# Gate and up products grouped by weight half, splits and additions pinned behind the mixers' chains, two loads held back, and a narrower last tile

## The chip, the cores and the metric

One core of one Trainium2 chip runs the whole program in a single launch. The metric is the device time of that launch in microseconds. Engines are named as in the profile: PE is TensorE (PEld its weight loads), DVE is VectorE, ACT is ScalarE, POOL is GpSimd, SP is SyncE, whose queue issues nearly all DMA transfers.

## The reference

A decoder trunk of two layers over one sequence: T = 256 tokens, D = 1024, all in float32. Each layer is a mixer and a SwiGLU network, each with a residual addition and an RMSNorm ahead of it; a last RMSNorm ends it.

```python
def rmsnorm(x, g):
    y = x * rsqrt(mean(x * x, -1) + 1e-6)
    return y * g
for layer in range(2):
    h = rmsnorm(x, norm_mix[layer])
    x = x + (even_mixer if layer == 0 else odd_mixer)(h)   # projection, attention branches, output projection
    h = rmsnorm(x, norm_ffn[layer])
    x = x + (silu(h @ w_gate) * (h @ w_up)) @ w_down       # D_FF = 2816
out = rmsnorm(x, norm_final)
```

The even mixer joins sparse attention with differential attention (two softmax maps a head, subtracted). The odd mixer joins compressed, selected and sliding-window attention in 16 heads of 64.

## The kernel before

**Products in halves.** Every large product is made from float32 numbers split into a high part `hi` (the value copied to the format fp32r) and a low part `lo` (the rest). A projection adds three products, hi·hi, hi·lo and lo·hi: `mm3`, lines 381 to 383 in the profile. In the gate and up products the activations stand side by side, 256 columns of hi and 256 of lo, in the tile `aW`. One product with the high weights (line 489) is therefore 512 wide, and one with the low weights (line 490) 256 wide, over the high columns only.

**Weights.** Class `Weights` brings the weights in tiles of 512 KB (`w_raw`, 4 buffers, by SP's queue, in the order of the program). ACT copies a tile to its high half `w_hi` (line 122) and DVE subtracts that to get `w_lo` (line 125); hi and lo have 7 buffers each. A tile of the gate or up weights holds 4 of the 8 steps over D, for 256 columns. `W.next()` hands out the next tile and makes splits some tiles ahead; `W.load` issues the transfers.

**The network (`ffn`).** Gate and up run in 11 chunks of 256 columns: 2 banks of gate (`ps_g`), 2 of up (`ps_u`), each bank 8 steps over D. Per step and bank comes one product of line 489 and one of line 490, in turn. After a chunk ACT and DVE add the two column halves, scale them (`rB`), apply Silu, multiply (`sg`, `hn`, lines 498 to 503) and split the result (`hT_hi`, `hT_lo`). `residual` then multiplies down, adds to x (line 435) and feeds the next norm.

**`residual` and `Norm`.** `residual` also makes the mixers' output projections. It runs over the last `tail` weight tiles bank by bank, so that the four quarters of x (two token tiles t by two column halves h) end one after the other. `amid` is called after the first quarter: in the even mixer it turns and splits the last attention output. After each quarter DVE adds to x (line 433, or 435 with a scale), `Norm.half` multiplies by the gain (`xg`, line 302), PE turns it (`pt_a`, line 278), and ACT and DVE split it into `aW` (lines 271, 272). `gain(...)` allots one shared buffer for a norm's gain and issues its transfer (line 203) on SP's queue; the buffer's last reader has to be done.

**Ends of the mixers.** In the odd mixer the last group of heads goes score, softmax (`softmax_terms`, lines 451 and 452), scaling by the sum (`e`, line 974), transposes (`pt_p`, line 979), products with the values (`ps_o`), split (`aT`). `cws`, a small table, is loaded at its head (line 784).

**`Final`.** It squares each quarter on ACT with a running sum (line 366), adds and takes the power −1/2 (DVE line 255, POOL), and scales the two output halves on ACT (line 375) and DVE (line 377).

**What sets the order.** The Tile framework's scheduler orders each engine's instructions by data and priority. `pin` (keep_in_program_order) fixes the order among the pinned. An engine works through its list in order, so an instruction that waits holds all behind it.

Of the kernel before, what the change touches and what calls it, by code (L numbers as in the profile page):

```python
# [15 lines left out]
D = 1024  # L16
# [65 lines left out]
class Weights:  # L82


    def __init__(self, tc, pool, rpool, lead, flats, specs, ahead, bufs, spare):
# [9 lines left out]
        self.ready = []  # L95
        self.used = 0

# [7 lines left out]
    def prepare(self, upto, behind=False, before=None):  # L105

        nc = self.tc.nc
        while len(self.ready) < min(upto, len(self.queue)):
# [8 lines left out]
            o = 0  # L117
            for j, part in enumerate(raw):
                if before:
                    before(j, len(raw))  # L120
                c = slice(o, o + part.shape[-1])
                act = nc.scalar.activation(hi[:, c], part, AF.Copy)  # L122
                if behind:
                    self.tc.keep_in_program_order(act)
                nc.vector.tensor_sub(lo[:, c], part, hi[:, c])  # L125
                o = c.stop
# [11 lines left out]
def trunk(tc, x, lead, w0, w1, sm0, cw, vec, cst, out, dbg=None):  # L138
# [107 lines left out]
    def evac(dst, src):  # L246
        A.activation(dst, src, AF.Copy)
# [21 lines left out]

    def split(hi, lo, src):  # L270
        A.activation(hi, src, AF.Copy)  # L271
        V.tensor_sub(lo, src, hi)  # L272

    def split_T(dst, k0, src, n, behind=False):

        pt = t_bank("pt_a").rearrange("p (k c) -> p k c", k=4)
        for i in range(n):
            mmi = TE.transpose(pt[:, i], src[:, i * P : (i + 1) * P], ident)
            if behind:
                pin(mmi)  # L280
        split(dst[0][:, k0 : k0 + n], dst[1][:, k0 : k0 + n], pt[:, :n])

    class Norm:


        def __init__(self, goff):
            self.goff = goff
            self.wide, self.aT = new_wide()
            self.rs = [small_tile(1, "rs") for _ in range(NT)]
            self.last = None  # L290
            self.ms = [None] * NT

        def finish(self):

            if self.last is not None:
                split_T(self.aT[NT - 1], 4, self.last, 4, behind=True)
                self.last = None

        def half(self, t, h):
# [3 lines left out]
            if (t, h) == (NT - 1, 1):  # L303
                self.last = xg
            else:
                split_T(self.aT[t], 4 * h, xg, 4)
# [48 lines left out]
    class Final:  # L355


        def __init__(self):
            self.ms = [small_tile(2, "ms2") for _ in range(NT)]
            self.y = [[nat("y") for _ in range(2)] for _ in range(NT)]  # L360

        def half(self, t, h):
            ms = self.ms[t]
            c = slice(512 * h, 512 * h + 512)
            sq = ap.tile([P, 512], BF16, tag="sq", bufs=2, name="sq")
            A.activation(sq, xs[t][:, c], AF.Square, scale=1.0 / math.sqrt(D), accum_out=ms[:, h : h + 1])
            V.tensor_mul(self.y[t][h], xs[t][:, c], gains[V_FIN][:, c])
            if h == 1:
                rf = small_tile(1, "ms")
                rsqrt_sum(rf, ms)  # L370
                for h in range(2):
                    c = slice(512 * h, 512 * h + 512)
                    y = self.y[t][h]
                    if h == 0:
                        A.activation(y, y, AF.Copy, scale=rf)
                    else:
                        V.tensor_scalar(y, y, rf, None, op0=ALU.mult)
                    (A, nc.sync)[h].dma_start(out[t * P : (t + 1) * P, c], y)

    def mm3(ps, act, k, wh, wl, start, stop):  # L380
        TE.matmul(ps, act[0][:, k], wh, start=start, stop=False)  # L381
        TE.matmul(ps, act[0][:, k], wl, start=False, stop=False)  # L382
        TE.matmul(ps, act[1][:, k], wh, start=False, stop=stop)  # L383
# [17 lines left out]
    def residual(act, nk, tail, nxt, rs=None, amid=None):  # L401

        ps = [[mm_bank("ps_out") for _ in range(2)] for _ in range(NT)]

        def one(t, h, k, wt):
            c = slice(512 * h, 512 * h + 512)
            mm3(ps[t][h], act[t], k, wt[0][:, 0, c], wt[1][:, 0, c], k == 0, k == nk - 1)
# [7 lines left out]
        if amid:  # L415
# [5 lines left out]
        for t, h, k0, k1 in order:  # L421
            c = slice(512 * h, 512 * h + 512)
            for k in range(k0, k1):
                one(t, h, nk - tail + k, last[k])
# [7 lines left out]
            if rs is None:  # L432
                V.tensor_add(xs[t][:, c], ps[t][h], xs[t][:, c])
# [15 lines left out]
    def softmax_terms(pool, s, m, scale, bias, e, den, n):  # L449

        V.tensor_tensor_reduce(e, s, m, -scale, 3e38, ALU.add, ALU.min, bias)  # L451
        A.activation(e, e, AF.Exp, scale=-1.0, bias=bias, accum_out=den)  # L452

    def ffn(nm, goff):
        wide, rs = nm.wide, nm.rs
        gain(goff)
        nxt = Final() if goff == V_FIN else Norm(goff)
        with tc.tile_pool(name="ffn", bufs=1, side="left", reuse_waits="tile") as fp:
# [18 lines left out]
            for w in FF_CHUNKS:  # L477
# [4 lines left out]
                for dst in (gp, up):  # L482
                    for g in range(KD // kk):
                        wh, wl = W.next()
                        for i in range(kk):
                            k = g * kk + i
                            for f in range(nf):
                                c = slice(f * P, (f + 1) * P)
                                TE.matmul(dst[f], wh[:, i, c], wide[:, k].rearrange("p z q -> p (z q)"), start=k == 0, stop=False)  # L489
                                TE.matmul(dst[f][:, :T], wl[:, i, c], wide[:, k, 0], start=False, stop=k == KD - 1)  # L490
# [14 lines left out]
                f0 += nf  # L505
            hT = [[z[:, :, t * P : (t + 1) * P] for z in (hh, hl)] for t in range(NT)]
# [665 lines left out]
```

## Time and profile before

| | |
|---|---|
| time, median of 3 runs | 659.0 us (657.96 to 659.56) |
| profiled execution | 660.14 us, span 658.4 us, mean granted clock 0.996 |
| even mixer, with its output projection | 0 to about 138 us |
| gate and up of the first network | 138 to about 263 us |
| down of the first network | to about 324 us |
| odd mixer, with its output projection | to about 466 us |
| gate and up of the second network | to about 590 us |
| down of the second network, and the end | to 658.4 us |

The profile is of one execution, and all places in it are in microseconds from the start of its span. "Busy" is the time in which an engine executes; products on PE overlap, so the step from one product's start to the next one's is what a product costs in a stream, and not its own duration.

### The profile page before, as it was taken

The page shows a single profiled execution, that of the slowest core. Times are in us where ns is not written, and L with a number is a line of the kernel's source. Part 1 is how long each engine was busy: PE and PEld are TensorE (multiplying, and loading weights), DVE is VectorE, ACT ScalarE, POOL GpSimd, SP SyncE. Part 2 cuts the span into 40 slices and gives each one's busy share as a digit, 9 for nine tenths or more (in the row PEclk, how much of TensorE's full clock was granted, in tenths as well). Part 3 has the DMA queues.
Part 4 walks back from the last instruction along what each step waited for, and adds up shares of the span by engine and source line. Part 5 has one row for each costly group of instructions (what it writes and reads, how often), then busy time and mean ns, then how long its engine had stood idle before and what let it go on. Part 6 is the DMA issues. An engine that isn't in the chain of part 4 may idle for free.

```text
span 658.4 us, 9972 instructions
## 1 busy us (share of the span) xinstructions
PE 644.2 (98%) x3508; PEld 538.1 (82%) x3508; DVE 485.9 (74%) x1094; ACT 396.3 (60%) x801; POOL 13.8 (2%) x26
## 2 busy tenths in 40 slices
PE   9999999999999999999999999999999999999995
PEld 6978788788888888888888877776888888888884
DVE  6799977759877787544579899796698777775424
ACT  7596757448655555433377598795585555554312
POOL 1100000000000000000000000000000000000000
PEclk9999999999999999999999999999999999999998
DMA  8943264147755566663197322410486565555501
GB/s 325 317 161 129 96 193 129 32 154 261 238 187 188 188 192 187 189 194 115 43 376 260 128 70 71 149 36 31 163 274 206 190 191 187 181 183 189 198 22 65
DMA packets 31729, 110.07 MB, mean 167 GB/s; under 512 B 3520, under 2 KB 3648, under 8 KB 31424
## 3 DMA queue, kind: packets, MB, share of 16 engines
q1 hardware_dynamic: 31392, 108.91, 50.3%
q8 instruction: 28, 0.46, 0.3%
q10 hardware_dynamic: 288, 0.52, 0.2%
q14 instruction: 21, 0.17, 0.1%
HBM read 108.37 MB, written 1.05 MB: 166 GB/s over the span
## 4 chain that ended last, share of the span: by engine, by line
PE 82%; DVE 5%; ACT 5%; DMA 4%; issue 2%; POOL 0%; SPq 0%; POOLq 0%; ACTq 0%
PE ps_u L489 12%; PE ps_g L489 11%; PE ps_out L381 7%; PE ps_out L383 7%; PE ps_out L382 7%; PE ps_u L490 6%; PE ps_g L490 6%; PE ps_in L382 5%; PE ps_in L381 5%; PE ps_in L383 5%; DMA w_raw<-in_w 3%; PE ps_o L995 2%; DVE w_lo L125 2%; PE ps_s L960 1%; PE pt_p L979 1%
## 5 line engine op out<-in xcount | busy, mean ns | idle before, releaser
L125 DVE TENSOR_TENSOR w_lo<-w_raw,w_hi 128x1024 fp32r<-128x1024 f32 (+4 forms) x196 | 232.0, 1189 | 88.3 <-ACT w_hi L122 85.9
L122 ACT ACTIVATE w_hi<-w_raw 128x1024 fp32r<-128x1024 f32 (+4 forms) x196 | 200.9, 1030 | 125.1 <-PE ps_out L383 56.7
L489 PE MATMUL ps_u<-aW,w_hi 128*128 128x512 f32 x352 | 125.6, 399 | 0.5 <-DVE hn L502 0.5
L489 PE MATMUL ps_g<-aW,w_hi 128*128 128x512 f32 x352 | 125.5, 399 | 0.3 <-DVE aW L272 0.3
L490 PE MATMUL ps_u<-aW,w_lo 128*128 128x256 f32 x352 | 98.8, 281 | 0.0
L490 PE MATMUL ps_g<-aW,w_lo 128*128 128x256 f32 x352 | 98.8, 281 | 0.0
L489 PEld LDWEIGHTS ps_g<-aW,w_hi 128*128 128x128 f32 x352 | 66.1, 188 | 17.2 <-DVE aW L272 0.9
L489 PEld LDWEIGHTS ps_u<-aW,w_hi 128*128 128x128 f32 x352 | 66.1, 188 | 17.1 <-DVE hn L502 0.8
L381 PE MATMUL ps_in<-w_hi,aW 128*128 128x512 f32 (+5 forms) x208 | 77.1, 374 | 0.9 <-ACT aW L271 0.8
L382 PE MATMUL ps_in<-w_lo,aW 128*128 128x512 f32 (+5 forms) x208 | 76.6, 369 | 0.3 <-DVE w_lo L125 0.3
L383 PE MATMUL ps_in<-w_hi,aW 128*128 128x512 f32 (+5 forms) x208 | 76.3, 368 | 0.0
L381 PE MATMUL ps_out<-w_hi,hT_hi 128*128 128x512 f32 x176 | 68.6, 390 | 0.0
L383 PE MATMUL ps_out<-w_hi,hT_lo 128*128 128x512 f32 x176 | 68.6, 390 | 0.0
L382 PE MATMUL ps_out<-w_lo,hT_hi 128*128 128x512 f32 x176 | 68.6, 390 | 0.0
L490 PEld LDWEIGHTS ps_g<-aW,w_lo 128*128 128x128 f32 x352 | 66.5, 189 | 0.0
L490 PEld LDWEIGHTS ps_u<-aW,w_lo 128*128 128x128 f32 x352 | 66.5, 189 | 0.0
L452 ACT ACTIVATE e<-e,bias 128x128 f32<-128x128 f32 (+1 forms) x96 | 42.5, 447 | 5.8 <-DVE bias L451 5.8
L381 PEld LDWEIGHTS ps_in<-w_hi,aW 128*128 128x128 f32 x208 | 39.2, 189 | 5.7 <-ACT aW L271 1.1
L382 PEld LDWEIGHTS ps_in<-w_lo,aW 128*128 128x128 f32 x208 | 39.3, 189 | 4.7 <-DVE w_lo L125 0.9
L383 PEld LDWEIGHTS ps_in<-w_hi,aW 128*128 128x128 f32 x208 | 39.2, 188 | 3.9 <-issue 0.2
L381 PEld LDWEIGHTS ps_out<-w_hi,hT_hi 128*128 128x128 f32 x176 | 33.1, 188 | 6.8
L383 PEld LDWEIGHTS ps_out<-w_hi,hT_lo 128*128 128x128 f32 x176 | 33.0, 188 | 6.8
(231 smaller groups left out, 895.8 us busy)
## 6 DMA issues: line engine op xcount, KB each, us to landing
w_raw<-in_w SPq DMA_DIRECT2D x176, 512.0 KB, 3.6
w_raw<-in_w SPq DMA_DIRECT2D x8, 384.0 KB, 4.3
gain<-in_vec SPq DMA_DIRECT2D x4, 512.0 KB, 4.4
cw<-in_cw SPq DMA_DIRECT2D x2, 1024.0 KB, 8.3
w_raw<-in_w SPq DMA_DIRECT2D x4, 416.0 KB, 8.8
w_raw<-in_w SPq DMA_DIRECT2D x4, 304.0 KB, 2.8
lead<-in_lead SPq DMA_DIRECT2D x2, 584.0 KB, 6.6
x<-in_x SPq DMA_DIRECT2D x4, 256.0 KB, 6.5
```

Source lines behind the costliest of these rows:

```text
L122: act = nc.scalar.activation(hi[:, c], part, AF.Copy)
L125: nc.vector.tensor_sub(lo[:, c], part, hi[:, c])
L381: TE.matmul(ps, act[0][:, k], wh, start=start, stop=False)
L382: TE.matmul(ps, act[0][:, k], wl, start=False, stop=False)
L383: TE.matmul(ps, act[1][:, k], wh, start=False, stop=stop)
L452: A.activation(e, e, AF.Exp, scale=-1.0, bias=bias, accum_out=den)
L489: TE.matmul(dst[f], wh[:, i, c], wide[:, k].rearrange("p z q -> p (z q)"), start=k == 0, stop=False)
L490: TE.matmul(dst[f][:, :T], wl[:, i, c], wide[:, k, 0], start=False, stop=k == KD - 1)
L960: mmi = TE.matmul(sb[:, i], qS[t][:, h], kz[:, par, :, :ns], start=z == 0, stop=z == 1)
L979: TE.transpose(pt[:, i, b, st], e[:, i, b, st * P : (st + 1) * P], ident)
L995: pin(TE.matmul(ob[64 * par : 64 * par + 64], vv[:, st, c : c + 64], pTs[par][:, b, st].rearrange("p j c -> p (j c)"), start=False, stop=l ...
```

## The change

- In `ffn`, all high products of a bank pair's step group come first and then all low ones: 16 and 16 (8 and 8 in the first chunk).
- In both networks the gain's load for the next norm is issued after the third chunk and not at the head; in the odd mixer `cws` is loaded after the first projection.
- `behind` adds an order between two instructions of one engine. With it, at the even mixer's end two low splits stand behind the last `pd`, the first addition to x behind the split of `aT`, and one further split behind that; the output projection's last tiles run quarter by quarter. At the odd mixer's end the first additions and five splits stand behind or ahead of named steps of the softmax, and the filler products of the second quarter behind the third. In that mixer `W.later = 100` gives splits a lower priority.
- In `Final`, the last quarter is computed in two banks of 256 columns, each added and squared by itself; sums are made by ACT (Identity with a bias), and the power is a square root on ACT and a reciprocal on DVE.

```diff
 class Weights
-            act = nc.scalar.activation(hi[:, c], part, AF.Copy)
-            nc.vector.tensor_sub(lo[:, c], part, hi[:, c])
+            with self.tc.high_priority(offset=-self.later):
+                    act = nc.scalar.activation(hi[:, c], part, AF.Copy)
+                    sub = nc.vector.tensor_sub(lo[:, c], part, hi[:, c])
+                self.parts.append((act, sub))
+    def behind(ins, other):
+        tc.add_manual_dep(ins.ins, other.ins.name, ...NoSync...)
 class Final
+        def square(self, t, o, n, last=False):
...
+            pin(A.activation(sq[:, :n], xs[t][:, o : o + n], AF.Square, scale=..., accum_out=ms[:, i : i + 1]))
+            if not last:
+                pin(A.activation(total, ms[:, i : i + 1], AF.Identity, bias=total))
+                if t == 0:
+                    A.activation(small_tile(1, "warm"), total, AF.Sqrt)
+            if last:
+                A.activation(self.rf, ms[:, i : i + 1], AF.Sqrt, bias=total)
+        def end(self, t):
+            V.reciprocal(rf, rf)
...
 def residual
+        if amid and not hold:
+            order = [(t, h, 0, tail) for t, h in ((0, 0), (0, 1), (1, 0), (1, 1))]
...
+            if isinstance(nxt, Final) and (t, h) == (NT - 1, 1):
+                px = t_bank("ps_x")
+                for q, (dst, o, n) in enumerate(((ps[t][h], 0, 256), (px, 256, 256))):
+                    for k in range(tail):
+                        mm3(dst[:, :n], act[t], nk - tail + k, ...)
+                    V.scalar_tensor_tensor(xs[t][:, cx], dst[...], rs[t], xs[t][:, cx], ...)
+                    nxt.square(t, cq.start, n, q == 1)
+                nxt.weigh(t, h)
+                nxt.end(t)
+                continue
...
 def ffn
-        gain(goff)
                 for dst in (gp, up):
+                    todo = []
                     for g in range(KD // kk):
-                        for i in range(kk):
-                            for f in range(nf):
-                                TE.matmul(dst[f], wh[:, i, c], wide[:, k]...)
-                                TE.matmul(dst[f][:, :T], wl[:, i, c], wide[:, k, 0]...)
+                        wt = W.next()
+                        todo += [(wt, i, g * kk + i, f) for i in range(kk) for f in range(nf)]
+                        if f0 and g < KD // kk - 1:
+                            continue
+                        for wt, i, k, f in todo:
+                            TE.matmul(dst[f], wt[0][:, i, ...], wide[:, k]...)
+                        for wt, i, k, f in todo:
+                            TE.matmul(dst[f][:, :T], wt[1][:, i, ...], wide[:, k, 0]...)
+                        todo = []
+                if f0 == 3 * nf:
+                    gain(goff)
 def even_mixer
+            for i in (8, 9):
+                behind(W.parts[o0 + i][1], mixed)      # mixed: the last pd
+            behind(nxt.added, parts[1])                # first addition to x; parts: split of aT
+            for part, ins in zip(W.parts[o0 + 10], parts):
+                behind(part, ins)
 def odd_mixer
-            tc.keep_in_program_order(nc.sync.dma_start(cws, cw[:, W1_N:]))
                 ps = project(aT, OD_CHUNKS[v], nm.finish)
+                if v == 0:
+                    tc.keep_in_program_order(nc.sync.dma_start(cws, cw[:, W1_N:]))
...
+            residual(oT, KD, 4, nxt, amid=lambda: None, gate=(scaled, copied), hold=True)
+            for i, first in ((5, (1, 0)), (6, (1, 0)), (7, (1, 1))):
+                for part, term in zip(W.parts[o0 + i], reversed(begun[first])):
+                    behind(term, part)
+            for i in (8, 9):
+                for part, ins in zip(W.parts[o0 + i], (copied, scaled)):
+                    behind(part, ins)
```

**PE, start of the first network.** Rows name the line, the instruction, output and inputs, shape, and how often it stands in a row. Before, from the last two products of the first gate half on:

```order
L489 MATMUL ps_g<-aW,w_hi 128x512
L490 MATMUL ps_g<-aW,w_lo 128x256
L278 MATMUL pt_a<-con,xg 128x128 x4
L473 MATMUL ps_r<-dg,ones 128x128 x2
L489 MATMUL ps_u<-aW,w_hi 128x512
L490 MATMUL ps_u<-aW,w_lo 128x256
```

Now, from the first gate product on:

```order
L555 MATMUL ps_g<-aW,w_hi 128x512 x8
L557 MATMUL ps_g<-aW,w_lo 128x256 x8
L285 MATMUL pt_a<-con,xg 128x128 x4
L538 MATMUL ps_r<-dg,ones 128x128 x2
L555 MATMUL ps_u<-aW,w_hi 128x512 x5
L555 MATMUL ps_g<-aW,w_hi 128x512 x8
L557 MATMUL ps_g<-aW,w_lo 128x256 x8
L555 MATMUL ps_u<-aW,w_hi 128x512 x3
L557 MATMUL ps_u<-aW,w_lo 128x256 x8
```

The alternation of lines 489 and 490 is gone; from the second chunk on the rows read 16 high and 16 low products throughout. Line 555 is the old 489, line 557 the old 490.

**SP, the queue of transfers from the even mixer's output projection to the odd mixer's head.** A tile of 128x1024 is 512 KB; `cw` is the small table, `cw_3420` a larger one. Before:

```order
L102 DMA w_raw<-in_w 128x1024 x18
L203 DMA gain<-in_vec 128x1024
L102 DMA w_raw<-in_w 128x1024 x6
L203 DMA gain<-in_vec 128x1024
L102 DMA w_raw<-in_w 128x1024 x62
L102 DMA w_raw<-in_w 128x608 x4
L784 DMA cw<-in_cw 128x224
L102 DMA w_raw<-in_w 128x512 x4
L102 DMA w_raw<-in_w 128x1024 x2
L800 DMA cw_3420<-in_cw 128x2048
```

Now:

```order
L104 DMA w_raw<-in_w 128x1024 x18
L207 DMA gain<-in_vec 128x1024
L104 DMA w_raw<-in_w 128x1024 x20
L207 DMA gain<-in_vec 128x1024
L104 DMA w_raw<-in_w 128x1024 x48
L104 DMA w_raw<-in_w 128x608 x4
L104 DMA w_raw<-in_w 128x512 x4
L104 DMA w_raw<-in_w 128x1024 x2
L876 DMA cw<-in_cw 128x224
L878 DMA cw_3420<-in_cw 128x2048
```

The second gain stands behind 14 more weight tiles, and `cw` behind 6 more; the weight tiles that followed them directly now go ahead of them.

**DVE, end of the odd mixer.** `e` is the scaled softmax, `den` its sums. Before:

```order
L125 TENSOR_TENSOR w_lo<-w_raw,w_hi 128x1024
L970 TENSOR_TENSOR den<-den,gates 128x2
L433 TENSOR_TENSOR x_82<-ps_out,x_82 128x512
L974 TENSOR_SCALAR e<-e,den 128x256 x2
L969 RECIPROCAL den<-den 128x2
L302 TENSOR_TENSOR xg<-x_82,gain 128x512
L970 TENSOR_TENSOR den<-den,gates 128x2
L433 TENSOR_TENSOR x_82<-ps_out,x_82 128x512
L974 TENSOR_SCALAR e<-e,den 128x256 x2
L272 TENSOR_TENSOR aT<-ps_o,aT 128x512
L272 TENSOR_TENSOR aW<-pt_a,aW 128x4x128
```

Now:

```order
L1050 TENSOR_TENSOR den<-den,gates 128x2
L1054 TENSOR_SCALAR e<-e,den 128x256 x2
L1049 RECIPROCAL den<-den 128x2
L1050 TENSOR_TENSOR den<-den,gates 128x2
L1054 TENSOR_SCALAR e<-e,den 128x256 x2
L495 TENSOR_TENSOR x_82<-ps_out,x_82 128x512
L312 TENSOR_TENSOR xg<-x_82,gain 128x512
L128 TENSOR_TENSOR w_lo<-w_raw,w_hi 128x1024 x3
L278 TENSOR_TENSOR aT<-ps_o,aT 128x512
L278 TENSOR_TENSOR aW<-pt_a,aW 128x4x128
L495 TENSOR_TENSOR x_83<-ps_out,x_83 128x512
```

The additions to x, the gain and the low splits moved from ahead of the last `e` to between it and the split of `aT`.

More of the change, by code (lines that the diff above doesn't have):

```diff
@@ L95, in __init__ @@
         self.ready = []
+        self.parts = []
         self.used = 0
+        self.later = 0
     def load(self, upto):
@@ L295, in finish @@
             if self.last is not None:
-                split_T(self.aT[NT - 1], 4, self.last, 4, behind=True)
+                split_T(self.aT[NT - 1], 4, self.last, 4, pinned=True)
                 self.last = None
@@ L358, in __init__ @@
         def __init__(self):
-            self.ms = [small_tile(2, "ms2") for _ in range(NT)]
+            self.ms = [small_tile(3, "ms3") for _ in range(NT)]
+            self.sum = [small_tile(1, "msum") for _ in range(NT)]
             self.y = [[nat("y") for _ in range(2)] for _ in range(NT)]
-        def half(self, t, h):
[L363 to L367, printed above, removed]
-            if h == 1:
[L369 to L383, printed above, removed]
+            self.part = [0] * NT
+            for total in self.sum:
+                G.memset(total, EPS)
+        def square(self, t, o, n, last=False):
+            i = self.part[t]
+            self.part[t] += 1
+            ms, total = self.ms[t], self.sum[t]
+            sq = ap.tile([P, 512], BF16, tag="sq", bufs=2, name="sq")
+            pin(A.activation(sq[:, :n], xs[t][:, o : o + n], AF.Square, scale=1.0 / math.sqrt(D), accum_out=ms[:, i : i + 1]))
+            if not last:
[3 more added lines that the diff above has]
+            if last:
+                self.rf = small_tile(1, "ms")
+                A.activation(self.rf, ms[:, i : i + 1], AF.Sqrt, bias=total)
@@ new lines, in weigh @@
+        def weigh(self, t, h):
+            c = slice(512 * h, 512 * h + 512)
+            V.tensor_mul(self.y[t][h], xs[t][:, c], gains[V_FIN][:, c])
+        def end(self, t):
+            rf = self.rf
+            V.reciprocal(rf, rf)
+            for h in range(2):
+                c = slice(512 * h, 512 * h + 512)
+                y = self.y[t][h]
+                if h == 0:
+                    A.activation(y, y, AF.Copy, scale=rf)
+                else:
+                    V.tensor_scalar(y, y, rf, None, op0=ALU.mult)
+                (A, nc.sync)[h].dma_start(out[t * P : (t + 1) * P, c], y)
@@ new lines, in half, with mm3 @@
+        def half(self, t, h):
+            self.square(t, 512 * h, 512, h == 1)
+            self.weigh(t, h)
+            if h == 1:
+                self.end(t)
+    def mm3(ps, act, k, wh, wl, start, stop, skip=False):
+        return (
+            TE.matmul(ps, act[0][:, k], wh, start=start, stop=False, skip_group_check=skip),
+            TE.matmul(ps, act[0][:, k], wl, start=False, stop=False, skip_group_check=skip),
+            TE.matmul(ps, act[1][:, k], wh, start=False, stop=stop, skip_group_check=skip),
+        )
@@ L422, in residual @@
             c = slice(512 * h, 512 * h + 512)
-            for k in range(k0, k1):
-                one(t, h, nk - tail + k, last[k])
+            if isinstance(nxt, Final) and (t, h) == (NT - 1, 1):
+                px = t_bank("ps_x")
+                for q, (dst, o, n) in enumerate(((ps[t][h], 0, 256), (px, 256, 256))):
+                    cq = slice(c.start + o, c.start + o + n)
+                    for k in range(tail):
+                        wt = last[k]
+                        mm3(dst[:, :n], act[t], nk - tail + k, wt[0][:, 0, cq], wt[1][:, 0, cq], q == 1 and k == 0, k == tail - 1, q == 0)
+                    cx = cq if q else c
+                    V.scalar_tensor_tensor(xs[t][:, cx], dst[:, : cx.stop - cx.start], rs[t], xs[t][:, cx], op0=ALU.mult, op1=ALU.add)
+                    nxt.square(t, cq.start, n, q == 1)
+                nxt.weigh(t, h)
+                nxt.end(t)
+                continue
+            for k in range(k0, k1):
+                made = one(t, h, nk - tail + k, last[k])
+                if hold and k0:
+                    for mmi in made:
+                        behind(mmi, column)
+                if inorder and (t, h, k) == (1, 0, 0):
+                    for mmi in nxt.turned[0, 0]:
+                        behind(mmi, made[-1])
+            if (t, h) == (1, 0):
+                column = made[-1]
+                if inorder:
+                    for mmi in nxt.turned[0, 1]:
+                        behind(mmi, column)
             if amid:
@@ L432, in residual @@
             if rs is None:
-                V.tensor_add(xs[t][:, c], ps[t][h], xs[t][:, c])
+                add = V.tensor_add(xs[t][:, c], ps[t][h], xs[t][:, c])
+                if (t, h) == (0, 0):
+                    nxt.added = add
+                if gate:
+                    behind(add, gate[0])
             else:
@@ L762, in even_mixer @@
                     if t and h0 == 0:
-                        split_T(oT[0], 4, ods[0], 4, behind=True)
+                        split_T(oT[0], 4, ods[0], 4, pinned=True)
                 rsqrt_eps(ssq, ssq)
@@ L1021, in trunk @@
     n = ffn(n, V_MIX1)
+    W.later = 100
     n = odd_mixer(n, V_FFN1)
+    W.later = 0
     ffn(n, V_FIN)
```

71 lines of the change are left out of this document (39 added, 32 removed).

## The prediction

> **What bounds the kernel now.** I read the page first, then the waits of PE, SP and DVE, the chain at each wait of PE, and timelines of PE inside the stages. The page's busy times:
>
> ```profile
> PE 644.2 (98%) x3508; PEld 538.1 (82%) x3508; DVE 485.9 (74%) x1094; ACT 396.3 (60%) x801; POOL 13.8 (2%) x26
> ```
>
> PE works 98% of the 658.4 us. Time can come from three places only: a shorter step between products, the 14 us in which PE does nothing, or the end, after its last product. The windows (length, then busy time and instructions of PE, PEld, DVE, ACT, POOL, granted clock, DMA share, GB/s) show where PE idles, and a steady stretch of gate and up:
>
> ```profile
> 128.00:139.00 11.00, 10.30 (x52) 7.98 (x52) 7.51 (x13) 3.78 (x10) 0.72 (x2) 1.00 0.01 1
> 160.00:264.00 104.00, 104.00 (x591) 90.21 (x590) 82.94 (x133) 61.37 (x113) 0.00 (x0) 1.00 0.64 198
> 324.00:344.00 20.00, 18.69 (x134) 17.30 (x133) 14.43 (x37) 13.57 (x27) 1.47 (x4) 1.00 0.83 311
> 645.00:658.40 13.40, 6.46 (x29) 5.02 (x27) 6.99 (x12) 4.35 (x10) 1.10 (x2) 0.83 0.21 78
> ```
>
> In gate and up PE never idles, DVE is 80% busy, the clock is full. At the seams it loses 0.7 and 1.3 us; before 139 no transfer runs, and after 324 the DMA engines are 83% busy.
>
> **Gate and up.** Durations overlap, so I price a product by the step from its start to the next start. The timeline in a steady stretch, and at the stage's start:
>
> ```profile
> 200.01 0.40 PE L489 MATMUL ps_g<-aW,w_hi 128*128 128x512 f32 x1
> 200.25 0.28 PE L490 MATMUL ps_g<-aW,w_lo 128*128 128x256 f32 x1
> ...
> 201.07 0.40 PE L489 MATMUL ps_g<-aW,w_hi 128*128 128x512 f32 x1
> ```
>
> ```profile
> 138.05 0.39 PE L489 MATMUL ps_g<-aW,w_hi 128*128 128x512 f32 x1
> ...
> 139.44 0.39 PE L489 MATMUL ps_g<-aW,w_hi 128*128 128x512 f32 x1
> ```
>
> From 200.01 to 201.07 lie three pairs of a high and a low product: 353 ns a pair. From 138.05 to 139.44 lie four: 347.5 ns. The faster step holds until PE's wait for `hn` (shown below, it ends at 156.81) and does not come back, in the second network neither; so some 52 of the 704 pairs are fast, (156.2 − 138.05) / 0.3475, and 650 slow. Streams of one width stand elsewhere: 512 wide in the down product, 256 wide in the odd projection:
>
> ```profile
> 643.82 0.39 PE L381 MATMUL ps_out<-w_hi,hT_hi 128*128 128x512 f32 x1
> ...
> 644.95 0.39 PE L383 MATMUL ps_out<-w_hi,hT_lo 128*128 128x512 f32 x1
> ```
>
> ```profile
> 334.78 0.28 PE L383 MATMUL ps_in<-w_hi,aW 128*128 128x256 f32 x1
> ...
> 335.98 0.28 PE L381 MATMUL ps_in<-w_hi,aW 128*128 128x256 f32 x1
> ```
>
> Five steps in 1.13 us are 226 ns, ten in 1.20 us are 120 ns. A pair in blocks then costs 227 + 120 = 347 ns, 6 less than 353: 650 × 6.3 ns = **−4.1 us**. One bound is no gain: the changes between blocks may cost, or the rate may not hang on the order (rival 1). The other is 1.4 us more, since the rows are rounded to 10 ns, about 1 ns on each of a pair's two steps (704 × 2 ns): −5.5. I take −4.1, since the two streams are products of the same widths in a row.
>
> The Trainium skill (TensorE: Matmul & The Clock Gate, "Back-to-back issue gap") gives N/2.4 + 2.5 ns for an isolated product, whatever its neighbours: 216 and 109, 325 a pair in either order. By it the regrouping is worth nothing; the trace's 226, 120 and 353 contradict its size.
>
> The buffers allow it. A block lasts 16 × 0.347 = 5.55 us and uses two tiles; the low halves are now freed at its end. With 7 buffers the split into a freed one is read 3 blocks on, at least 10 us later, and takes DVE about 1.2 us.
>
> **The seams.** PE's waits, then SP's (engine, line, releaser: total, times, longest, in us):
>
> ```profile
> PE pt_p L979 <- DVE e L974: 1.0, 1, 1.0
> PE ps_in L381 <- ACT aW L271: 0.8, 1, 0.8
> PE pt_a L278 <- DVE xg L302: 0.7, 1, 0.7
> ...
> PE ps_u L489 <- DVE hn L502: 0.5, 1, 0.5
> PE pt_f L822 <- ACT F L247: 0.5, 1, 0.5
> ...
> PE ps_g L489 <- DVE aW L272: 0.3, 1, 0.3
> ```
>
> ```profile
> SPq L203 <- DVE rs L255: 46.5, 2, 24.3
> SPq L784 <- PE ps_out L382: 17.6, 1, 17.6
> ```
>
> Even mixer's end, `pt_a` 0.7. The chain (start, length, what) goes through a low split and then the addition to x:
>
> ```profile
> 126.85 0.30 DVE w_lo L125
> ...
> 127.90 0.69 DVE x L433
> ```
>
> The change puts one split behind that addition and two others behind the last `pd`: **−0.7** (bounds 0, and −0.7 for the wait). The output quarters now run in order, with as many products as before.
>
> First network, `ps_u` 0.5:
>
> ```profile
> 140.12 5.38 DMA w_raw<-in_w
> ...
> 155.19 1.22 DVE w_lo L125
> ...
> 156.81 0.50 PE ps_u L489
> ```
>
> The gain's transfer waited 24.3 us for the norm's `rs` and held the weight tiles on SP's queue; the order shows 14 that now go ahead of it, as far as their 4 raw buffers reach: **−0.5** (bounds 0, and −0.5 for the wait). The gain's own transfer is needed by nothing on PE until the next norm, in the down stage.
>
> Odd mixer's head, `ps_in` 0.8 and `pt_f` 0.5:
>
> ```profile
> 326.16 3.88 DMA w_raw<-in_w
> ...
> 333.25 8.94 DMA w_raw<-in_w
> ```
>
> `cws` waited 17.6 us for a product of the down stage, with the odd weights behind it. Now four tiles of 256 KB, 1.05 MB, pass it, some 3.4 us at this window's 311 GB/s. The first wait should go; the second belongs to the full DMA stage, which starts that much earlier: **−1.2** of 1.3 (bounds 0, −1.3).
>
> Odd mixer's end, `pt_p` 1.0 and `ps_g` 0.3:
>
> ```profile
> 449.00 1.12 DVE w_lo L125
> ...
> 451.38 0.59 DVE xg L302
> ...
> 452.64 0.27 DVE e L974
> ...
> 453.05 0.41 PE pt_p L979 x2
> ...
> 458.28 0.61 ACT aT L271
> ```
>
> The split, the gain step and the additions stand ahead of the last `e`; now they follow it. There they have to fit beside the transposes, the products `ps_o` and ACT's half of `aT`, from 452.91, where `e` ends, to 458.89: 5.98 us. They are an addition, a gain step and three low splits, 2 × 0.7 + 3 × 1.22 = 5.1 us. That fits by 0.9 us, and products of the output projection stand behind as filler. **−1.2** (bounds +1.0, if the splits run late and `aT` waits, and −1.3).
>
> The seams together: −0.7 − 0.5 − 1.2 − 1.2 = **−3.6** (bounds +1.0 and −3.8).
>
> **The end.** The last product, and what follows it:
>
> ```profile
> 651.07 0.39 PE L383 MATMUL ps_out<-w_hi,hT_lo 128*128 128x512 f32 x1
> 651.63 0.74 DVE L435 SCALAR_TENSOR_TENSOR x<-ps_out,rs,x 128x512 f32<-128x512 f32 x1
> 652.41 0.63 ACT L366 ACTIVATE sq<-x 128x512 bf16<-128x512 f32 x1 [0.66 <-DVE x L435]
> 653.46 0.55 POOL L256 TENSOR_TENSOR ms<-ms,half 128x1 f32<-128x1 f32 x1 [3.65 <-DVE ms L255]
> 654.04 0.72 ACT L375 ACTIVATE y<-y,ms 128x512 f32<-128x512 f32 x1 [0.91 <-POOL ms L256]
> ```
>
> From 651.07 to 654.04 are 2.97 us. Now the last quarter is 18 products of 256 (18 × 120 = 2.16 us against 9 × 227 = 2.04: +0.12). A last addition and square half as wide, 0.37 and 0.32 less by their rows at most, and no POOL step, 0.55 against a root and a reciprocal, could save up to 1.0. But ACT works in order: the first half's output (0.72), its issue, a square of 512 (0.63 and its sum), two of 256, two sums and the root now stand in one row. By estimate, from 649.46, where the third quarter's last product ends (651.07 − 9 × 0.227 + 0.4): addition 0.75, reciprocal 0.2, output and issue 1.2, squares 0.75 + 2 × 0.5, sums and root 3 × 0.25, reciprocal 0.3: the last `y` starts at 654.4. **+0.4** (bounds −1.0 and, with sums twice as long, +1.1). Sqrt needs one more table load, priced by the row of the others (2 loads, mean 1283 ns):
>
> ```profile
> L500 ACT ACT_TABLE_LOAD x2 | 2.6, 1283 | 0.0
> ```
>
> It falls between the squares of the first two quarters, beside PE's 2.0 us of products a quarter, which cover it. By the Trainium skill (ScalarE: Activation LUTs, "What ACT_TABLE_LOAD costs") a switch also has a drain of 1.38 us, 2.66 in all; no row here shows a drain behind a load. With it the next square would come 0.7 us late, and the third quarter's work would take that up.
>
> **Sum.** 660.14 − 4.1 − 3.6 + 0.4 = 652.8 for the profiled execution, whose span is 658.4 with 1.7 us around it. It is 1.1 above the median of 659.0, so the runs should come to **651.7 us**.
>
> **Rivals.**
> 1. *The order doesn't set the rate.* At the start the same alternation ran at 347 ns, so the slow rate may be a state that a disturbance leaves behind, and blocks may lock into a slow step too. For it: two rates with one order. Against: both single-width streams settle within a few products after each wait. Gate and up give 0: 659.0 − 3.6 + 0.4 = 655.8.
> 2. *The seams give nothing*: the waits are replaced by others, since the same splits must be done within the same few microseconds, and the end loses 0.4. For it: DVE at 80% and DMA at 83%. 659.0 − 4.1 + 0.4 = 655.3. Both together: 659.0 + 0.4 = 659.4, no change.
> 3. *Slower: paired release starves gate and up.* Low buffers free in pairs, after a block, and DVE's rows come in pairs; when a split must wait for a block's end, DVE loses up to 1.8 us a block, since a block's first low half is free after 16 × 0.227 + 8 × 0.12 = 4.6 us and not after 8 × 0.353 = 2.8. Against that stands DVE's reserve of 20% × 5.55 = 1.1 us. The missing 0.7 us in 42 blocks is 29 us on top of 651.7: 681. It decides from 0.18 us a block on (7.3 / 42). Against it: the 10 us of lead worked out above.
>
> **How the numbers follow.** My forecast (gate and up near −4, most of the seams) 0.60; rival 1 0.15; rival 2 0.12; both together 0.08; rival 3 0.05. The range goes from 648.5 (659.0 − 5.5 − 3.8 − 1.0 = 648.7) to 657.0, which takes in rivals 1 and 2 each alone, with the end at its bound. About 0.3% (2 us) is what measurements of this kernel can tell apart: faster 0.87, same 0.08, slower 0.05.
>
> **What would show it.** Steps of 227 and 120 in gate and up, from 138 on, without an initial wait at 156; no waits of `ps_in` L381 and `pt_a`; SP's gain wait gone; the last `e` ahead of the additions, with `aT` ready when `ps_o` ends; the last `y` about 3.3 us after the last product starts. I would be wrong if a pair in blocks costs 353 as well, if PE waits on `w_lo` inside gate and up, or if `pt_a` at the odd mixer's end now waits for the three splits.

## The result, and the profile after

The changed kernel takes 652.81 us (median of 6 runs, 652.55 to 652.95) against 659.53 us for the kernel before (6 runs, 657.96 to 661.48). The ratio is 0.9893, 95% interval 0.9874 to 0.9912. The forecast was 651.7, in a range of 648.5 to 657.0. The profiled execution took 652.77 us with a span of 651.0: 7.4 us less than before.

The page's busy times, and its chain by engine:

```profile
PE 641.0 (98%) x3517; PEld 539.3 (83%) x3517; DVE 476.0 (73%) x1095; ACT 403.0 (62%) x810; POOL 12.4 (2%) x26
PE 92%; ACT 4%; DVE 2%; issue 1%; POOL 0%; ACTq 0%
```

The chain of before, by engine:

```profile
PE 82%; DVE 5%; ACT 5%; DMA 4%; issue 2%; POOL 0%; SPq 0%; POOLq 0%; ACTq 0%
```

It is now PE almost throughout, and DMA has left it. PE's waits, all that the view names:

```profile
PE warm_ps L226 <- DVE warm L221: 1.2, 1, 1.2
PE ps_s L1039 <- DVE dn L1010: 0.6, 1, 0.6
PE pt_c L651 <- DVE n L648: 0.3, 1, 0.3
PE ps_i L675 <- ACT rel L677: 0.2, 1, 0.2
PE pt_f L900 <- ACT nk L895: 0.2, 1, 0.2
```

The waits of the four seams are gone but for 0.2 us of `pt_f`; what remains stood there before. SP's list has no wait for `rs` and none for a product of the down stage any more. The windows, in the columns of before, at the even mixer's end, in steady gate and up, and at the odd mixer's head:

```profile
128.00:139.00 11.00, 11.00 (x54) 8.56 (x54) 9.09 (x14) 5.50 (x13) 0.72 (x2) 1.00 0.16 49
160.00:264.00 104.00, 104.00 (x598) 91.85 (x598) 77.53 (x134) 64.63 (x116) 0.00 (x0) 1.00 0.58 200
324.00:344.00 20.00, 19.81 (x133) 18.02 (x132) 16.93 (x47) 16.26 (x30) 0.70 (x2) 1.00 0.83 322
```

PE is busy without a gap in the first, where transfers now run before 139, and loses 0.2 in place of 1.3 us in the third. To place the 7.4 us, the first product of each stage, from PE's timeline of before (the first gate product, 138.05, and the last product, 651.07, stand in the prediction):

```profile
263.97 0.40 PE L381 MATMUL ps_out<-w_hi,hT_hi 128*128 128x512 f32 x1
...
325.26 0.30 PE L381 MATMUL ps_in<-w_hi,aW 128*128 128x304 f32 x1
...
466.04 0.50 PE L489 MATMUL ps_g<-aW,w_hi 128*128 128x512 f32 x1 [0.28 <-DVE aW L272]
...
591.39 0.40 PE L381 MATMUL ps_out<-w_hi,hT_hi 128*128 128x512 f32 x1
```

and of after:

```profile
137.47 0.45 PE L555 MATMUL ps_g<-aW,w_hi 128*128 128x512 f32 x1
...
260.98 0.40 PE L414 MATMUL ps_out<-w_hi,hT_hi 128*128 128x512 f32 x1
...
322.29 0.30 PE L414 MATMUL ps_in<-w_hi,aW 128*128 128x304 f32 x1
...
460.37 0.39 PE L555 MATMUL ps_g<-aW,w_hi 128*128 128x512 f32 x1
...
583.91 0.40 PE L414 MATMUL ps_out<-w_hi,hT_hi 128*128 128x512 f32 x1
...
643.77 0.28 PE L416 MATMUL ps_x<-w_hi,hT_lo 128*128 128x256 f32 x1
```

| stage (differences of these starts, us) | before | after | difference |
|---|---|---|---|
| to the first gate product | 138.05 | 137.47 | −0.58 |
| gate and up, first network | 125.92 | 123.51 | −2.41 |
| down, first network | 61.29 | 61.31 | 0.0 |
| odd mixer | 140.78 | 138.08 | −2.70 |
| gate and up, second network | 125.35 | 123.54 | −1.81 |
| down, second network, to the last product | 59.68 | 59.86 | +0.18 |
| from the last product to the end of the span | 7.3 | 7.2 | −0.1 |

A block in the timeline, which joins equal products in a row, so that a block is one row:

```profile
199.75 3.82 PE L555 MATMUL ps_u<-aW,w_hi 128*128 128x512 f32 x16
203.40 2.08 PE L557 MATMUL ps_u<-aW,w_lo 128*128 128x256 f32 x16
205.31 0.63 PE L555 MATMUL ps_g<-aW,w_hi 128*128 128x512 f32 x2
```

Sixteen high products take 3.65 us from start to start (228 ns each), sixteen low ones 1.91 (119): 347.5 ns a pair. From the third chunk on, the first five high steps of a block are the slow ones (means 233, 236, 228, 232 and 231 ns, then 227), and the first two low steps are 113 and 119 ns, the rest 120. A return to high products so costs 27 ns, of which the low steps give 7 back. From the second chunk on a chunk of 32 pairs takes 11.13 us, 347.8 ns a pair.

The odd mixer's end on DVE:

```profile
445.20 0.62 DVE L1054 TENSOR_SCALAR e<-e,den 128x256 f32<-128x256 f32 x2
445.74 0.69 DVE L495 TENSOR_TENSOR x<-ps_out,x 128x512 f32<-128x512 f32 x1
446.45 0.69 DVE L312 TENSOR_TENSOR xg<-x,gain 128x512 f32<-128x512 f32 x1
447.94 3.50 DVE L128 TENSOR_TENSOR w_lo<-w_raw,w_hi 128x1024 fp32r<-128x1024 f32 x3 [0.80 <-ACT w_hi L125]
451.49 0.69 DVE L278 TENSOR_TENSOR aT<-ps_o,aT 128x512 fp32r<-128x512 f32 x1
```

The addition, the gain step and the three low splits follow the last `e`, and the split of `aT` starts as soon as they end. PE has products of the output projection to do meanwhile and does not wait.

The end, from the chain of the work that ended last (start, length, what):

```profile
642.79 0.73 ACT y L401
...
643.55 0.37 ACTq L404
...
643.97 0.73 ACT sq L381 x2
...
646.17 0.30 ACT ms L388
...
646.50 0.17 DVE ms L396
...
646.70 0.72 ACT y L401
```

The narrower last tile brings nothing, and the chain suggests why. The last output step starts 2.93 us after the last product's start, against 2.97 before. Its chain no longer begins at the last product: it runs along ACT's list, through the first tile's output, its issue, three squares, two sums and the root.

### The profile page after: what moved, and what is told of

Read it like the earlier page. It is cut to its first block, busy times and chain, and to the rows that moved or that the text cites. A ratio compares the mean times of both kernels' runs of the same rounds, so it can differ in the third digit from the quotient of the medians.

```text
span 651.0 us, 9989 instructions
## 1 busy us (share of the span) xinstructions
PE 641.0 (98%) x3517; PEld 539.3 (83%) x3517; DVE 476.0 (73%) x1095; ACT 403.0 (62%) x810; POOL 12.4 (2%) x26
## 4 chain that ended last, share of the span: by engine, by line
PE 92%; ACT 4%; DVE 2%; issue 1%; POOL 0%; ACTq 0%
PE ps_g L555 12%; PE ps_u L555 12%; PE ps_out L416 8%; PE ps_out L415 8%; PE ps_out L414 8%; PE ps_u L557 6%; PE ps_g L557 6%; PE ps_in L414 6%; PE ps_in L415 6%; PE ps_in L416 6%; PE ps_o L1075 2%; PE pt_p L1059 2%; PE ps_s L1039 2%; PE pt_a L285 1%; PE ps_s L752 1%; PE warm_ps L226 1%
## 5 line engine op out<-in xcount | busy, mean ns | idle before, releaser
L555 PE MATMUL ps_u<-aW,w_hi 128*128 128x512 f32 x352 | 84.9, 392 | 0.0
L555 PE MATMUL ps_g<-aW,w_hi 128*128 128x512 f32 x352 | 84.5, 391 | 0.0
L415 PE MATMUL ps_out<-w_lo,hT_hi 128*128 128x512 f32 (+1 forms) x176 | 68.3, 388 | 0.0
L414 PE MATMUL ps_out<-w_hi,hT_hi 128*128 128x512 f32 (+1 forms) x176 | 68.3, 388 | 0.0
L416 PE MATMUL ps_out<-w_hi,hT_lo 128*128 128x512 f32 (+1 forms) x176 | 68.3, 388 | 0.0
L557 PEld LDWEIGHTS ps_u<-aW,w_lo 128*128 128x128 f32 x352 | 45.4, 191 | 1.9
L557 PEld LDWEIGHTS ps_g<-aW,w_lo 128*128 128x128 f32 x352 | 45.4, 191 | 1.9
L557 PE MATMUL ps_u<-aW,w_lo 128*128 128x256 f32 x352 | 46.0, 283 | 0.0
L557 PE MATMUL ps_g<-aW,w_lo 128*128 128x256 f32 x352 | 46.0, 283 | 0.0
L415 PEld LDWEIGHTS ps_out<-w_lo,hT_hi 128*128 128x128 f32 x176 | 33.1, 188 | 6.7
```

The source lines that it names most:

```text
L414: TE.matmul(ps, act[0][:, k], wh, start=start, stop=False, skip_group_check=skip),
L415: TE.matmul(ps, act[0][:, k], wl, start=False, stop=False, skip_group_check=skip),
L416: TE.matmul(ps, act[1][:, k], wh, start=False, stop=stop, skip_group_check=skip),
L555: TE.matmul(dst[f], wt[0][:, i, f * P : (f + 1) * P], wide[:, k].rearrange("p z q -> p (z q)"), start=k == 0, stop=False)
L557: TE.matmul(dst[f][:, :T], wt[1][:, i, f * P : (f + 1) * P], wide[:, k, 0], start=False, stop=k == KD - 1)
```

## Experiments

**Is it the order of the products?** The kernel before with the regrouping alone:

```diff
 before, in ffn
-  high, low, high, low, ... (one pair per step and bank)
+  16 high products, then 16 low ones (8 and 8 in the first chunk)
```

> The kernel before with the regrouping of gate and up alone (16 high products, then 16 low ones). If the order of the products sets their step, both gate/up stages shorten by about 1.8 us each without the rest of the change, 3.5 us in all: the ratio to the kernel before is 0.9945 and the wait for hn near 156 stays at 0.5 us. If the order does not set the step and the shorter stages came from quieter seams, nothing moves (ratio 1.000).

Measured: 657.11 us, ratio 0.9949 (0.9931 to 0.9966). Gate and up take 124.24 us in the first network (−1.68) and 123.49 in the second (−1.86), a gain of 3.5 us without the rest of the change, and with PE's wait for `hn` near 156 still there. The odd mixer took 1.0 us more in this profile, so its span is only 2.2 us shorter. The same edit the other way round, in the changed kernel:

```diff
 after, in ffn
-  16 high products, then 16 low ones
+  high, low, high, low, ...
```

> The changed kernel with the old alternation of high and low products, everything else as changed. If the order sets the step: 3.5 us above the changed kernel's 652.8, so 656.3, the steady pair back at 353 ns and the second network's gate/up stage at 125.3 us in place of 123.5. If the step is a state that a stall leaves behind, then, with the wait at 156 gone, the pair stays at 346.5 ns and the time is 652.8 or less.

Measured: 654.36 us, 1.6 above the changed kernel, not 3.5. Neither expectation holds, because each describes one of the two networks. Two starts of chunks, 32 pairs apart, in the first network and then in the second:

```profile
160.56 0.40 PE L554 MATMUL ps_g<-aW,w_hi 128*128 128x512 f32 x1
...
171.66 0.40 PE L554 MATMUL ps_g<-aW,w_hi 128*128 128x512 f32 x1
...
494.96 0.40 PE L554 MATMUL ps_g<-aW,w_hi 128*128 128x512 f32 x1
...
506.26 0.40 PE L554 MATMUL ps_g<-aW,w_hi 128*128 128x512 f32 x1
```

11.10 and 11.30 us: 347 and 353 ns a pair. The alternation ran in the fast step through the whole first network (123.19 us, 0.3 less than the blocks). In the second (125.38) it began fast as well, at 346 to 347 ns, and was slow after the 0.9 us of other products near 462.7. So the order alone does not set the step: the alternation has two.

**What picks the step?** In the next kernel the alternation is back, and one small product after each chunk moves the start of the next; nothing reads its result.

```diff
 the run before, in ffn, after each chunk
+  TE.matmul(t_bank("ps_n")[:, :width], ones, ones[:, :width], start=True, stop=True)
+  # width = 11 * chunk (first network), 11 * chunk - 6 (second), chunk from 1
```

> The changed kernel with the old alternation, and after each chunk of gate and up one extra float32 product of a width that grows by 11 columns a chunk (11 to 121 in the first network, 5 to 115 in the second); its result is used nowhere. It only shifts the moment at which the next chunk's alternation starts. Theory L, locked cycles: the alternation falls after each interruption into one of two repeating patterns by its phase; the mean pair step, read chunk by chunk, is near 347 ns in some chunks and near 353 in others, in both networks. Theory N, the second network is slow for a reason of its own (its neighbours, its place in the program): all chunks of the first network at 347, all of the second at 353. The extra products and restarts cost about 0.25 us each, 5 us in all: near 660.

Measured: 660.31 us, one run. The first and the last high product of two neighbouring chunks in the first network:

```profile
161.63 0.48 PE L554 MATMUL ps_g<-aW,w_hi 128*128 128x512 f32 x1
...
172.66 0.40 PE L554 MATMUL ps_u<-aW,w_hi 128*128 128x512 f32 x1
...
173.16 0.47 PE L554 MATMUL ps_g<-aW,w_hi 128*128 128x512 f32 x1
...
184.00 0.40 PE L554 MATMUL ps_u<-aW,w_hi 128*128 128x512 f32 x1
```

11.03 and 10.84 us for the same 31 pairs and their restart. Over all chunks, the last twelve pairs of a chunk have a mean of 346.7 ns (8 of the 22 chunks) or 353.3 (14), nothing between, four fast chunks in each network. That is theory L: after an interruption the alternation settles to one of two steps and keeps it until the next one. "Cycle" here stands for the mean of a repeating pattern; the slow one repeats every three pairs (350, 350, 360 ns).

In one more kernel only the first network alternates. Its tail, and "the run before" of its expectation, are those of the kernel with both of the first token tile's scalings on POOL, told under the end:

> The run before (first token tile's scaling on POOL) with the old alternation in the first network alone and blocks in the second. If the alternation locks into the fast cycle again in the first network, as in the run with alternation throughout, its gate/up stage takes 123.2 us in place of 123.5 and the time is 0.3 us under the run before: 651.9. If its phase comes out otherwise, 125.3 us and 654.

Measured: 654.90 us, 1.9 above the run with the same tail and blocks in both networks. The first network took 125.50 us, every chunk from the second on at 353 ns. PE's instructions, and their order, are the same up to there as in the run that alternated throughout, where it took 123.19. The cycle is therefore not fixed by the order of the products; what decides it is open.

**Shorter and longer blocks.**

```diff
 after, in ffn
-  16 high, 16 low
+  2 high, 2 low, ...
```

> The changed kernel with blocks of two: two high products, two low ones, in turn. Theory S, settling: after a low product the first six high steps run over 227 ns (by 11, 9, 2, 5, 3 and 3 in the changed kernel) and the first low step 6 under 120; then a pair costs 347 + (11 + 9 - 7)/2 = 353 ns, as much as in strict alternation, and the second network's gate/up stage takes 125.3 us. Theory C, each change of width costs the same: half as many changes halve the 6.3 ns, a pair costs 350 ns and the stage takes 124.3 us.

Measured: 653.35 us. From the third chunk on both networks run at 11.15 us a chunk, 348.3 ns a pair: neither theory's number. Theory S was also worked out from wrong steps: its means mix in the restarts of the first chunk, and with those of steady blocks (7 and 9 over, 7 and 1 under) it gives 351 and not 353. A fixed price gives 350. The steps (233, 236, 116, 113, 232, 231, 113, 119) fit neither: the excess depends on what came before. Blocks of two already avoid the slow cycle. The second network's stage took 124.21 us, since PE stopped once, for 0.4 us, near 478.

```diff
 after, in ffn, from the second chunk on
-  gate: 16 high, 16 low; up: 16 high, 16 low
+  gate 16 high, up 16 high, gate 16 low, up 16 low
```

> The changed kernel with gate and up joined in each chunk: 32 high products, then 32 low ones (from the second chunk on). Theory S: a block's settling of about 27 ns is paid half as often, 20 times less in each network: the second network's gate/up stage is 0.5 us shorter (123.0 us), the whole 652.8 - 1.0 = 651.8. Theory C: 0.15 us shorter in each. Rival, the release of four tiles' low halves at a time starves PE: waits of ps_g or ps_u on w_hi or w_lo appear in the steady stage, and 20 chunks with 0.2 us each cost 4 us.

Measured: 653.26 us. A chunk takes 11.11 us in place of 11.13: 20 ns for the one return to high products saved, which is the 27 less 7 ns read above. The expectation counted 20 returns saved in each network; there are ten, one a chunk, so 0.2 us and not 0.5. The first network's stage was 0.18 us shorter, the second's 0.45 longer, by one wait of `ps_u`:

```profile
PE ps_u L549 <- DVE hn L583: 0.4, 1, 0.4
```

It is the finishing of the first chunk on DVE that comes late there, once, and not the release of low halves: `hn` stands on DVE behind the low split of a weight tile whose transfer took 6.07 us. The stall in blocks of two has the same chain, with a transfer of 6.68 us. It is the chain of the wait near 156 before, here with the gain's load out of the way. Neither this run nor the changed kernel has a wait on `w_hi` or `w_lo` inside steady gate and up.

**The seams, one part taken back at a time.** Each was run once, and is read from its profile.

```diff
 after
+  gain(goff) at the head of ffn; cws loaded at the head of odd_mixer
-  gain(goff) after the third chunk; cws loaded after the first projection
```

> The changed kernel with the two loads back where they were: each network's gain at the head of the network, cws at the head of the odd mixer. If their place on SP's queue made the waits at 156 and 330: SP waits 24 us on rs and 17 us on a down product again, the first gate/up stage takes 124.2 us in place of 123.5, the odd mixer is about 1.2 us longer, and the span is 651.0 + 1.9 = 652.9 us. Rival: the splits' new order alone keeps PE fed; then the waits on SP come back and PE's do not, and the span stays at 651.0.

Measured: 655.34 us, span 653.6. PE's and SP's waits:

```profile
PE ps_in L414 <- ACT aW L278: 0.8, 1, 0.8
PE ps_u L556 <- DVE hn L571: 0.7, 1, 0.7
```

```profile
SPq L207 <- DVE rs L259: 51.8, 2, 30.4
...
SPq L860 <- PE ps_out L415: 17.5, 1, 17.5
```

The odd mixer is 1.2 us longer (139.25 us), as expected. The stall of `ps_u` came in the second network, near 480, where before it was in the first: that stage takes 124.53 us, 1.0 more. The first takes 123.77, only 0.26 more and not the 0.7 expected. The chain at the wait near 480, in parts, goes through SP's issue of the gain:

```profile
463.91 0.00 SPq L207
...
464.01 5.48 DMA w_raw<-in_w
...
480.55 0.35 DVE hn L571
```

So the gain's transfer was a risk at both networks. The margin there is thin: runs with the late gain lost up to 0.7 us at the same place. Why the stall moved from the first network to the second is not shown, nor what else in the change removed the rest of it in the first, where the regrouping alone, with the old seams, took 0.73 us more than the changed kernel. Together with 0.2 us of earlier drift this is the 2.6 us.

```diff
 even_mixer
-  behind(...): two splits behind the last pd, the first addition behind aT, one split behind that
-  quarters in order
+  no fixed order; quarters as before
```

> The changed kernel with the even mixer's end as before: no fixed order of the splits and of the first addition to x, and the old order of the last quarters. If a low split ahead of the addition made pt_a wait: that wait of 0.7 us is back near 128, the first gate product starts at 138.2 in place of 137.47 and the span is 651.7. Rival: the wait had gone with the other changes; then 651.0.

Measured: 653.73 us, span 652.0; the output projection takes 33.59 us in place of 32.88, and the wait is back. The split, the addition and the order of the quarters went back together, so the share of each is not shown:

```profile
PE pt_a L285 <- DVE xg L312: 0.7, 1, 0.7
```

```diff
 odd_mixer
-  W.later = 100; gate=(scaled, copied); behind(...) on five splits and the softmax
+  none of these
```

> The changed kernel with the odd mixer's order left to the scheduler: no fixed order at its end, no lower priority for the splits in it. If the splits, the addition and the gain step ahead of the last e made pt_p wait: that wait of about 1.0 us is back, with 0.3 to 1 us of short waits behind it, the odd mixer takes 140 us in place of 138.1 and the span is 652.8. Rival: the early start of the odd weights alone made the gain; then 651.3 or less.

Measured: 654.58 us, span 652.8; the odd mixer takes 139.86 us, 1.78 more, with these waits back. The three parts went back together and are not told apart:

```profile
PE pt_p L1059 <- DVE e L1054: 1.1, 1, 1.1
...
PE ps_g L555 <- DVE aW L278: 0.3, 1, 0.3
```

**The end.**

```diff
 Final and the last quarter
-  two banks of 256, sums and root on ACT, reciprocal on DVE
+  one bank of 512, sums on DVE, power on POOL (as before)
```

> The changed kernel with the old end: the last quarter in one bank, sums on DVE, power on POOL. If ACT's row of work holds the new end, as the chain of the changed kernel shows, then the new end gains nothing: the last product starts 0.18 us earlier, the time from it to the end is 7.3 us in place of 7.2, and the span is 650.9. If the narrower last tile is worth what half an addition, half a square and POOL's step cost, 652.0.

Measured: 653.28 us, span 651.4. Down takes 59.64 us (−0.22) and the end 7.28 (+0.06): the old end is 0.16 us shorter by these two stages; the other 0.6 us of this one execution lie ahead of it, in stages that the edit does not touch. The new end is worth nothing here. Is ACT's list the reason?

```diff
 Final.end, first token tile
-  y[0] on ACT, y[1] on DVE; y[0] issued on ACT's queue
+  both on POOL, issued on SP's queue
```

> The changed kernel with the first token tile's last scaling on POOL, and its output issued on SP's queue, in place of ACT, DVE and ACT's queue. If ACT's row of work holds the end, the square of the third quarter starts right after its addition, at 642.7 in place of 643.97, and the last y starts 0.6 us earlier (2.3 us after the last product's start in place of 2.93); the time is 652.8 - 0.6 = 652.2. If another chain (DVE's additions, the first tile's outputs from a slow POOL) ends last, the same or more.

Measured: 653.04 us (652.43 to 653.41). ACT was the holder of the last y: it starts at 645.65, 2.13 us after the last product (643.52) in place of 2.93. But the end still comes 7.45 us after it:

```profile
642.68 3.92 POOL L401 TENSOR_SCALAR y<-y,ms 128x512 f32<-128x512 f32 x2 [179.80 <-DVE ms L396]
```

POOL needs 1.96 us for each half, until 646.60, and SP's queue issues the last tile's second half behind them, until 647.45. The end comes 3.5 us after that issue, as it came 3.4 us after SP's last one in the changed kernel (647.56). So I left one half on POOL:

```diff
 the run before
-  y[1] of the first token tile on POOL, both issued on SP's queue
+  y[1] on DVE again; y[0] issued on POOL's queue
```

> The changed kernel with only the first half of the first token tile's last scaling on POOL, issued on POOL's own queue; the second half stays on DVE. In the run with both halves on POOL one took 1.96 us there and the last y started 2.13 us after the last product's start, but the first tile's outputs then ended last. If ACT's row holds the end, and one POOL step of 2 us ends early enough (644.7), the last y starts 2.45 us after the last product's start in place of 2.93 and the end comes 6.75 us after it in place of 7.22: 652.8 - 0.5 = 652.3. If the last output transfers take as long whenever they start, 652.8.

Measured: 653.01 us (652.77 to 653.18), the end 7.40 us after the last product:

```profile
643.20 1.91 POOL L401 TENSOR_SCALAR y<-y,ms 128x512 f32<-128x512 f32 x1 [179.81 <-DVE ms L396]
...
643.58 0.92 DVE L405 TENSOR_SCALAR y<-y,ms 128x512 f32<-128x512 f32 x1
```

DVE's scaling took 0.92 us beside POOL's, against 0.48 before. With it in front, the last two additions came late, and the last y started 2.96 us after the last product. No version here is measurably faster than the changed kernel.

## Why the prediction was right, and where not

- **Sum of the profiled execution.** Forecast 652.8, measured 652.77. The terms, against the table of stages and the parts taken back: gate and up −4.1 forecast, −4.22 in the two stages, of which 0.67 is the stall near 156 (a step of 0.795 there in place of 0.12), so −3.55; that stall −0.5 forecast, −0.67 measured; even mixer −0.7 against −0.71 (taken back alone; −0.58 in the table); odd mixer −2.4 against −2.70 (1.2 from the loads, 1.8 from its order, by the parts taken back, which overlap by 0.3); the end +0.4 against +0.1. That the sum fits to 0.1 us is in part luck: gate and up fell 0.55 short, and the other terms together came out about that much better.
- **The level was off by 1.1 us** (651.7 against 652.81). The step that failed is the last one of the sum: that the runs would stand 1.1 below the profiled execution because they did before. After the change, they do not (652.77 against 652.81). The offset was most likely chance: over the 33 runs of the kernel before beside the changed kernel and these experiments, on several chips, from 657.96 to 663.11, the median is 660.2, so the profiled 660.14 was an ordinary execution and the median of three, 659.0, a low one. In the six runs beside the changed kernel's own, the kernel before spreads over 3.5 us, the changed one over 0.4. Two parts of the change bear on that: with the alternation back, the same kernel's four runs spread from 653.66 to 656.55; with the regrouping alone and the old seams, from 655.84 to 658.17. That either part makes the scatter is not shown.
- **Gate and up: right in size, half right in reason.** A pair in blocks costs 347.8 to 347.9 ns, against 347 forecast, and a slow one 353. The missing 0.55 us comes from the return to high products, 20 ns in each of some 40 blocks, which the sum put at nothing. (Of the pairs counted as fast, 52, only 47 were: the count took the 0.9 us of other products near 140.7 for pairs. It changes the term by 0.03 us.) But the prediction took the alternation for slow by its order. It is slow only in one of its two cycles. In the first network the alternation without the stall near 156 once kept the fast one (123.19 us against 123.51 with blocks) and once had the slow one (125.50). Rival 1 had this mechanism, with the wrong conclusion: blocks of 2, 16 and 32 have no slow cycle in any of these profiles. What blocks buy is the certain step. The Trainium skill's formula for an isolated product (TensorE: Matmul & The Clock Gate, "Back-to-back issue gap") has no order and no phase in it; an estimate by it is 325 ns a pair. Here the step was 346.7 or 353.3 for one and the same order.
- **Seams: right.** Rival 2 fell: no wait took the place of those removed. The splits at the odd mixer's end are done at 451.44, where ACT's half of `aT` is (451.46).
- **The loads: right in mechanism, short in reach.** I gave −0.5 at the first network; taken back, the loads cost 1.3 us in the two networks together, 1.0 of it in the second, where the kernel before had no stall to show. In the first they account for 0.26 us of the 0.7 alone.
- **The end: right in mechanism, for the last y.** ACT's list does hold that step: the chain shows it, and with the list relieved it came 0.8 us sooner, though that edit relieved DVE as well. Whether the end would follow it is not shown: in both kernels that relieved ACT another chain held it. The last y starts 2.93 us after the last product, against 3.2 by the sum (654.4 less 651.19; "about 3.3" in the forecast's signs). From the end of the third quarter's last product it took 4.80 us (641.90 to 646.70) and not 4.94, and the last quarter's products took 0.1 us more than worked out. The one more table load took its 1.28 us, from 639.72; the step behind it began at 641.01, and the third quarter's work took the delay up, as forecast.
- **Rival 3 did not occur**: no wait on a low half in steady gate and up, even with four tiles released at once.

## What to carry to other kernels

Where an in-order engine stalls at a seam, look at what stands ahead of the late instruction in its list: a split, an addition or a load that nobody needs yet. Moving it behind the chain is worth the whole wait, if the engine that was waited for still has the time afterwards. Give a product stream equal blocks (two of a kind were enough here), and read a stream's step in several places of one trace before calling it the price of its order. Do not carry the offset between one profiled execution and the median over to another kernel: with three runs of a kernel that scatters over 3.5 us it can be chance, and the scatter itself may go with the change.

## What the runs showed of the hardware that was not expected

- High products 512 wide alternating with low ones 256 wide lock into one of two cycles, 346.7 or 353.3 ns a pair at a granted clock of 1.00, and keep it over hundreds of products until an interruption. With the same order on PE, one kernel had the fast cycle in a whole stage, another the slow one. The fast mean came in two patterns: 347, 347, 346 ns in the kernel before, 350, 343, 350, 343, 350, 344 in the changed kernel with the alternation.
- After a run of narrower products the first five wide ones take up to 236 ns in place of 227, and the first narrow one after a wide run 113 in place of 120.
- POOL needs 1.9 us to scale a tile of 128x512, DVE 0.48. Beside POOL the same step on DVE once took 0.92 us; with POOL's second half in flight in the other kernel it took 0.48. What decides that is open.
